# S5 layer of a decoder trunk: each group of channels gets its own 64x64 quarter of the array, and rows of u, K and y are moved by DMA through DRAM

## The chip, the cores and the metric

The kernel runs on one core of a Trainium2 chip. The metric is the device time of one execution, in microseconds (us).

## The reference, cut to what matters

The trunk has two layers over 256 positions of 2048 channels. The second layer's mixer runs a sliding-window attention beside an S5 state-space layer. S5 has 64 groups of 16 channels; each group has 64 complex states of its own, so no group reads another group's channels:

```python
u32 = u.reshape(b, s, 64, 16)                                  # 64 groups of 16 channels
a_bar = exp(lam * dt);  b_bar = ((a_bar - 1) / lam) * b_mat    # per group: 64 states
bu = einsum('bsgc,gpc->bsgp', u32, b_bar)                      # complex
state = linear_scan(a_bar, bu)                                 # over the positions
y = einsum('bsgp,gcp->bsgc', state, c_mat).real + d_skip * u32
z = gelu(y)
return z * sigmoid(z @ glu_w + glu_b)
```

Everything else (projections, attention, the other layer, the two feed-forward blocks) is dense work that the change leaves as it is.

## The kernel before, in words

**Dense work.** Each projection runs in groups. A group loads its weights as 1 MB tiles `w` on the one DMA queue that the kernel uses, that of SyncE (SP), from a pool of six buffers (`WB`) that the `ada` tiles share. ScalarE (ACT) rounds each half of a tile to `hi` (L330), VectorE (DVE) takes the rest as `lo` (L331), four buffers of each, and TensorE (PE) runs three matmuls for each 128x128 piece (helper `mm`, L138): hi times the activation's high part, hi times its low part, lo times its high part. One group of the odd layer's input projection has 96 of these matmuls, one of its output projection or of the GLU 48. A `step` emits a group and then what belongs beside it: DVE's work on the `ada` tiles, and chains of smaller work that advance one piece per slot. A scheduler turns this into one fixed instruction order for each engine before the run; each engine then works strictly in that order, and so does each DMA queue.

**S5.** Four positions are handled at a time: u is regrouped so that a partition is a position in the block of four and a channel, 32 channels (two groups) by 4 positions on 128 partitions, 64 blocks along the free axis. One unit i = 0 to 7 covers 128 channels as four sub-units t. All S5 matmuls are float32, with 128x128 weights that hold two groups of channels side by side; the other group's half of each is zero. A float32 matmul shows in the trace as two records.
- `s5_tables` (L1125) makes the weights of unit i from the parameters, during the first layer's feed-forward block (`ffn(0)`): powers of A on DVE, masked copies on ACT (L1151, L1152, L1163), eight transposes (L1171) copied by L1172, twelve matmuls with 32 columns, and ten copies of 32 partitions (L1188) that lay out the convolution kernel K. L836 spills the five tables of a unit to DRAM, 256 KB each, on SP's queue.
- `s5_states` (L1210) runs eight matmuls with 64 columns for unit i, then a chain of fourteen DVE operations (two scans among them) that gives `hs`, the states.
- `s5_outputs` (L1249) runs twelve matmuls on u, `hs` and the tables and copies the result to `y` (L1259).
- `s5_load` regroups u by sixteen ACT copies of 32 partitions (L939) for each pair of units; `s5_store` does the same from y to z (L961). L972 brings six tables of a unit back, on SP's queue.
- `s5_all` issues, in slot n, the table loads of unit n, the states of unit n-1 and the outputs of unit n-2. It starts when the first u is there. The odd input projection's groups come in the order `OD_ORDER = 'uqqqquuu'` behind the first (k and v), and the S5 work lies between their matmuls and those of the attention's output projection (`od_out`). Rows of a query group are moved between partitions by four DMAs (L585).

After the attention's part of `od_out`, z goes through a gelu (L1003) and is split into high and low part (L318, L319); then come the GLU's four groups, which read all eight pieces of z in order, and the S5 half of `od_out`.

Of the kernel before, what the change touches and what calls it, by code (L numbers as in the profile page):

```python
# [27 lines left out]
U_DMA = False  # L28
Z_DMA = False
# [66 lines left out]
def trunk(ctx: ExitStack, tc: tile.TileContext, a: dict, out: bass.AP):  # L96
# [525 lines left out]
    s5d = [[dp.tile([P, 512], F32, name=f"s5_{i}_{j}") for j in range(6)] for i in range(8)]  # L622
# [140 lines left out]
    for i in range(8):  # L763
        beside[steps[0] + TURN_AT[i]] = lambda i=i: DMA.dma_start(s5d[i][5], s5_turn(nc, s5w, i))
# [166 lines left out]

    def s5_load(g, ps):

        if not U_DMA:
            us[g] = t2((P, 2, 4, 64))
            un = ps.rearrange("p m (c j) -> p m j c", j=4)
            for t in range(4):
                for q in range(4):
                    S.copy(us[g][32 * q:32 * q + 32, :, t, :], un[32 * t:32 * t + 32, :, 3 - q, :])  # L939
# [6 lines left out]
    def turn_rows(src, dst, g):  # L946

        d = dp.tile([P, 2, 4, 64], F32, name=nm("rows"))
        DMA.dma_start(d, src)
        dst[g] = t2((P, 2, 4, 64))  # L950
        for b in range(4):
            DMA.dma_start(dst[g][32 * b:32 * b + 32], d.rearrange("(a r) m b c -> r b m a c", a=4)[:, b])

    def s5_store(g):
        if Z_DMA:
            turn_rows(ys[g], zs, g)
            return
        zs[g] = t2((P, 2, 4, 64))
        for t in range(4):
            for j in range(4):  # L960
                S.copy(zs[g][32 * t:32 * t + 32, :, j, :], ys[g][32 * j:32 * j + 32, :, t, :])  # L961

    def s5_all():

        tabs, hs = {}, {}
        for n in range(10):
            while n < 8 and n // 2 not in us:
                yield
            if n < 8:
                tabs[n] = [t2() for _ in range(6)]  # L970
# [74 lines left out]
def cmul(V, o_re, o_im, ar, ai, br, bi, tmp):  # L1045
# [79 lines left out]
def s5_tables(nc, w, i, pss, mm):  # L1125
    V, S, G, PE = nc.vector, nc.scalar, nc.gpsimd, nc.tensor
    t1, t2, sm, a, par, ident = (w[k] for k in ("t1", "t2", "sm", "a", "par", "ident"))
    ts = slice(4 * i, 4 * i + 4)

    def powers(k0, k1, x):  # L1130
# [13 lines left out]
    d = powers(1, 4, (craw[:, 0], craw[:, 1]))  # L1144
    c0 = t1((P, 2, 4, 2, 16))
    ckf = [t2() for _ in range(2)]
    ck = [v.rearrange("p (t k e c) -> p t k e c", t=4, k=4, e=2) for v in ckf]
# [6 lines left out]
    b0, tmp = [sm((P, 4, 16)) for _ in range(2)], sm((P, 4, 16))  # L1154
    fr, fi = (w["f"][:, r, ts].unsqueeze(2).to_broadcast([P, 4, 16]) for r in (0, 1))
    cmul(V, b0[0], b0[1], fr, fi, craw[:, 2], craw[:, 3], tmp)
    d = powers(1, 3, b0)
    bk = []
    for r in range(2):
        S.copy(d[r][:, :, 0, :], b0[r])  # L1160
# [226 lines left out]
```

## Time and profile before

| | before |
|---|---|
| median of 3 runs | 2244.04 us (2243.14 to 2247.28) |
| the profiled execution's own time | 2243.86 us |
| its span in the trace | 2242.0 us |
| PE / PE's weight loads / DVE / ACT busy | 97% / 88% / 83% / 56% |
| mean granted TensorE clock | 0.985 of full speed |
| DMA, mean busy share, and rate | 73.3%, 274 GB/s |

The profiled execution takes 1.86 us more than its span, and lies inside the three runs. A busy share is a mean over stages with different limits. PE's records are pipelined and overlap, so the step from one record's start to the next (its pitch), not its duration, is what it takes of PE's time.

### The profile page before, as it was taken

How to read it: one execution, taken by the hardware profiler on the slowest of the kernel's cores; microseconds unless marked ns; L12 is line 12 of the kernel's file. 1: busy time of each engine (PE TensorE's matmuls, PEld its weight loads, DVE VectorE, ACT ScalarE, POOL GpSimd, SP SyncE). 2: the span in 40 equal slices, each digit the busy share in tenths (PEclk: the TensorE clock that was granted, in tenths of full speed). 3: DMA queues.
4: the chain of work that ended last, by engine and by line, in shares of the span. 5: the costliest groups of instructions: out<-in, count | busy, mean ns of one | idle time of the engine just before them, and what ended most of it. 6: DMA issues, size and time to landing. Idle time of an engine off the chain costs nothing. (4 is left out here: it accounts for less than half of the span.)

```text
span 2242.0 us, 36822 instructions
## 1 busy us (share of the span) xinstructions
PE 2181.0 (97%) x14266; PEld 1981.4 (88%) x14266; DVE 1867.4 (83%) x3104; ACT 1257.1 (56%) x2188; POOL 4.4 (0%) x12
## 2 busy tenths in 40 slices
PE   7999999999999999999999999999999999999997
PEld 4799989998988888888888999999989888888886
DVE  7789999989999869999988778986799757877765
ACT  3355856445776456655544777644566444555543
POOL 0000000000000000000000000000000000000000
PEclk9999999999999999999999999999999999999999
DMA  8997689888768977788876757878755768655651
GB/s 341 383 347 295 237 310 354 323 351 302 283 228 307 359 300 311 305 322 333 326 283 202 288 210 270 301 242 294 291 188 203 258 228 307 244 188 188 205 195 71
DMA packets 106066, 615.05 MB, mean 274 GB/s; under 512 B 12065, under 2 KB 14625, under 8 KB 54817
## 3 DMA queue, kind: packets, MB, share of 16 engines
q1 hardware_dynamic: 105890, 612.69, 73.3%
q8 instruction: 112, 1.84, 0.3%
q14 instruction: 64, 0.52, 0.1%
HBM read 592.72 MB, written 18.87 MB: 273 GB/s over the span
## 5 line engine op out<-in xcount | busy, mean ns | idle before, releaser
L138 PE MATMUL mm<-t,hi 128*128 128x256 f32 (+1 forms) x4720 | 1213.5, 324 | 11.1 <-ACT hi L393 4.3
L138 PEld LDWEIGHTS mm<-t,hi 128*128 128x128 f32 x4720 | 795.3, 192 | 64.9 <-ACT hi L393 4.7
L138 PE MATMUL mm<-t,lo 128*128 128x256 f32 x3168 | 846.1, 285 | 3.6 <-DVE lo L331 3.5
L331 DVE TENSOR_TENSOR lo<-w,hi 128x1024 fp32r<-128x1024 f32 (+1 forms) x558 | 654.6, 1183 | 188.2 <-ACT hi L330 177.8
L330 ACT CAST hi<-w 128x1024 fp32r<-128x1024 f32 (+1 forms) x558 | 561.9, 1017 | 419.6 <-PE sp L138 268.4
L138 PE MATMUL sp<-t,hi 128*128 128x512 f32 (+1 forms) x2448 | 789.2, 357 | 0.0
L138 PEld LDWEIGHTS mm<-t,lo 128*128 128x128 f32 x3168 | 606.7, 192 | 24.0 <-DVE lo L331 5.5
L138 PE MATMUL sp<-t,lo 128*128 128x256 f32 x2032 | 523.4, 283 | 0.0
L138 PEld LDWEIGHTS sp<-t,hi 128*128 128x128 f32 x2448 | 436.9, 190 | 53.3 <-ACT hi L393 0.2
L221 DVE CUSTOM_DVE_ANT_0 ada<-ada,cond 128x2048 f32<-128x2048 f32 x192 | 438.4, 2285 | 10.5 <-DMA ada<-in_adaT 6.5
L138 PEld LDWEIGHTS sp<-t,lo 128*128 128x128 f32 x2032 | 389.0, 192 | 16.4
L393 ACT CAST hi<-w 128x768 fp32r<-128x768 f32 (+2 forms) x160 | 146.8, 922 | 168.7 <-PE sx L138 89.3
L394 DVE TENSOR_TENSOR lo<-w,hi 128x768 fp32r<-128x768 f32 (+2 forms) x160 | 167.7, 1062 | 63.3 <-ACT hi L393 61.0
L797 DVE SCALAR_TENSOR_TENSOR t<-t,ffn_p,t 128x255 f32<-128x255 f32 (+1 forms) x344 | 148.8, 480 | 11.3 <-ACT t L795 9.5
L795 ACT ACTIVATE t<-t,ffn_p 128x256 f32<-128x256 f32 x172 | 93.5, 594 | 51.8 <-DVE t L787 43.7
L291 ACT ACTIVATE t<-t,mods 128x256 fp32r<-128x256 f32 x64 | 30.0, 506 | 84.1 <-DVE mods L311 61.8
L138 PE MATMUL sx<-t,t 128*128 128x64 f32 (+2 forms) x480 | 68.3, 283 | 2.4 <-DMA t<-s 1.3
L138 PEld LDWEIGHTS sx<-t,t 128*128 128x128 f32 x480 | 61.8, 194 | 4.7 <-DMA t<-s 1.6
L318 ACT CAST t<-t 128x256 fp32r<-128x256 f32 x102 | 40.3, 404 | 42.9 <-DVE t L801 36.6
L138 PE MATMUL mm<-t,w 128*128 128x256 f32 x256 | 56.5, 380 | 0.9 <-ACT t L695 0.9
L264 ACT ACTIVATE t<-x 128x256 f32<-128x256 f32 x80 | 31.8, 414 | 44.3 <-DVE x L469 25.7
L138 PEld LDWEIGHTS mm<-t,w 128*128 128x128 f32 x256 | 48.5, 190 | 7.8 <-ACT t L695 1.3
(272 smaller groups left out, 1525.7 us busy)
## 6 DMA issues: line engine op xcount, KB each, us to landing
ada<-in_adaT SPq DMA_DIRECT2D x192, 1024.0 KB, 6.1
w<-in_ffn_in SPq DMA_DIRECT2D x116, 1024.0 KB, 5.6
w<-in_ffn_out SPq DMA_DIRECT2D x80, 896.0 KB, 4.6
w<-in_ffn_first SPq DMA_DIRECT2D x48, 896.0 KB, 6.1
w<-in_ev_out SPq DMA_DIRECT2D x16, 1024.0 KB, 6.5
w<-in_ffn_out SPq DMA_DIRECT2D x16, 1024.0 KB, 5.1
w<-in_od_out SPq DMA_DIRECT2D x16, 1024.0 KB, 6.9
w<-in_ev_a SPq DMA_DIRECT2D x16, 896.0 KB, 6.7
```

The costliest lines, as they stand in the source:

```text
L138: keep(PE.matmul(o, l, r, start=start, stop=stop, skip_group_check=True))
L221: V.tensor_tensor_reduce(out=w, in0=w, in1=cond, scale=1.0, scalar=0.0, op0=ALU.mult, op1=ALU.add, accum_out=mods[l][:, j:j + 1])
L264: S.activation(sq, x[i], AF.Square)
L291: S.activation(o[:, 0, :], t, AF.Identity, bias=sh[:, i:i + 1])
L318: S.copy(o[:, 0, :], src)
L330: S.copy(hi[:, :m], w[:, o:o + m])
L331: V.tensor_tensor(lo[:, :m], w[:, o:o + m], hi[:, :m].bitcast(F32), op=ALU.subtract)
L393: S.copy(hi[:, :c], w[:, o:o + c])
L394: V.tensor_tensor(lo[:, :c], w[:, o:o + c], hi[:, :c].bitcast(F32), op=ALU.subtract)
L795: S.activation(c, ps[s], AF.Identity, bias=fp[:, 3, j:j + 1], scale=fp[:, 2, j:j + 1])
L797: V.scalar_tensor_tensor(c[:, d:], ps[s][:, :T - d], fp[:, 2 - d, j:j + 1], c[:, d:], op0=ALU.mult, op1=ALU.add)
```

## The change

Every S5 matmul is cut into 64x64 quarters: one group's rows against one group's columns, for the upper half (partitions 0 to 63) and the lower half (64 to 127) in turn. There are twice as many S5 matmuls for states and outputs, each a quarter of the size. The zero halves are gone, so the tables take 512, 512, 256 and 512 columns in place of six times 512. Rows no longer lie in 32s that ACT can copy between partitions; u and y are written whole to DRAM and read back by eight DMAs of 16 partitions each (`turned`), and K is written as 128x112 and copied inside DRAM by sixteen DMAs for each unit. ACT makes four copies of 128 partitions for u and none for y.

```diff
     def s5_table(i):
-        tabs = yield from s5_tables(nc, s5w, i, psx, mm)
-        for d, t in zip(s5d[i], tabs):
-            DMA.dma_start(d, t)
+        bT, c5, kz = yield from s5_tables(nc, s5w, i, psx, mm)
+        DMA.dma_start(s5d[i][0], bT)
+        for r in range(2):
+            DMA.dma_start(s5d[i][1].rearrange("p (r t s) -> p r t s", r=2, t=4)[:, r],
+                          c5[r][:, :, 1:5, :].rearrange("p t k c -> p t (k c)"))
+
+        zd = dp.tile([P, 112], F32, name=nm("kz"))
+        DMA.dma_start(zd, kz.rearrange("p k c -> p (k c)"))
+        dst = s5d[i][2].rearrange("(e q c) (t s) -> q t e c s", e=2, q=4, t=4)
+        src = zd.rearrange("(t e c) s -> t e c s", t=4, e=2)
+        for q in range(4):
+            for t in range(4):
+                DMA.dma_start(dst[q, t], src[t, :, :, 16 * q:16 * q + 64])
...
+    def turned(src, view, dst, rows):
+
+        d = dp.tile([P, 2, 4, 64], F32, name=nm("rows"))
+        DMA.dma_start(d, src)
+        v = d.rearrange(view, r=16, **rows)
+        for n in range(8):
+            DMA.dma_start(dst[16 * n:16 * n + 16], v[n // v.shape[1], n % v.shape[1]])
+
     def s5_load(g, ps):

...
         un = t2((P, 2, 4, 64))
         for q in range(4):
             S.copy(un[:, :, q, :], ps.rearrange("p m (c j) -> p m j c", j=4)[:, :, 3 - q, :])
-        turn_rows(un, us, g)
...
+        us[g] = t2((P, 2, 4, 64))
+        turned(un, "(t e r) m q c -> e q r m t c", us[g], dict(t=4, e=2))
 
     def s5_store(g):
-        if Z_DMA:
-            turn_rows(ys[g], zs, g)
-            return
         zs[g] = t2((P, 2, 4, 64))
-        for t in range(4):
-            for j in range(4):
-                S.copy(zs[g][32 * t:32 * t + 32, :, j, :], ys[g][32 * j:32 * j + 32, :, t, :])
+        turned(ys[g], "(e j r) m t c -> t e r m j c", zs[g], dict(e=2, j=4))
...
     def s5_all():
...
-                tabs[n] = [t2() for _ in range(6)]
+                tabs[n] = [t2()[:, :v.shape[1]] for v in s5d[n]]
...
 def s5_tables(nc, w, i, pss, mm):
...
         for e in range(2):
-            m = par[:, 1 + r, e:e + 1]
-            S.activation(ck[r][:, :, :, e, :], d[r], AF.Copy, scale=m)
-            S.activation(c0[:, r, :, e, :], craw[:, r], AF.Copy, scale=m)
...
-    for r in range(2):
-        S.copy(d[r][:, :, 0, :], b0[r])
-        o = t2((P, 4, 4, 2, 16))
-        for e in range(2):
-            S.activation(o[:, :, :, e, :], d[r], AF.Copy, scale=par[:, 1, e:e + 1])
-        bk.append(o)
+            S.activation(bp[:, r, :, e, :], b0[r], AF.Copy, scale=par[:, 1, e:e + 1])
     for _ in range(YIELDS):
         yield
-    bT = [t2() for _ in range(2)]
+
+    tp = pss().rearrange("p (r t s) -> p r t s", r=2, t=4)
     for r in range(2):
-        tp = pss()
         for t in range(4):
-            PE.transpose(tp[:, t * P:(t + 1) * P], bk[r][:, t].rearrange("p k e c -> p (k e c)"), ident)
-        S.copy(bT[r], tp)
-
-    dd = sm((P, 4, 32))
-    V.tensor_tensor(dd, w["eye"].unsqueeze(1).to_broadcast([P, 4, 32]),
-                    w["d"][:, ts].unsqueeze(2).to_broadcast([P, 4, 32]), op=ALU.mult)
-    kps = pss().rearrange("p (t c) -> p t c", t=4)
-    for t in range(4):
-        mm(kps[:, t, 0:32], ident, dd[:, t, :], True, False)
-        for r in range(2):
-            mm(kps[:, t, 0:32], bk[r][:, t].rearrange("p k e c -> p (k e c)"),
-               c0[:, r, t].rearrange("p e c -> p (e c)"), False, r == 1)
-    kTf = t2()
-    kT = kTf.rearrange("p (t j c) -> p t j c", t=4, j=4)
-    G.memset(kTf, 0.0)
-    for k in range(4):
-        for q in range(k, 4):
-            S.copy(kT[32 * q:32 * q + 32, :, k + 3 - q, :], kps[32 * k:32 * k + 32, :, 0:32])
-    return *bT, *ckf, kTf
+            for h in (slice(0, 64), slice(64, 128)):
+                mm(tp[h, r, t, :], bk[r][h, t].rearrange("p k c -> p (k c)"), ident[h, h], True, True)
+    bT = t2()
+    S.copy(bT.rearrange("p (r t s) -> p r t s", r=2, t=4), tp)
+
+    kps = pss()
+    for r in range(2):
+        for t in range(4):
+            mm(kps[32 * t:32 * t + 32, 0:64], bp[:, r, t].rearrange("p e c -> p (e c)"),
+               c5[r][:, t, 0:4, :].rearrange("p k c -> p (k c)"), r == 0, r == 1)
+    kz = sm((P, 7, 16))
+    G.memset(kz[:, 0:3, :], 0.0)
+    V.scalar_tensor_tensor(kz[:, 3, :], w["eye"], w["d"][:, i:i + 1], kps[:, 0:16], op0=ALU.mult, op1=ALU.add)
+    S.copy(kz[:, 4:7, :].rearrange("p k c -> p (k c)"), kps[:, 16:64])
+    return bT, c5, kz
...
 def s5_states(nc, w, i, u, tabs, pss, mm, pin):
...
     for r in range(2):
         for t in range(4):
-            mm(vps[:, r, t, :], bT[r][:, t, :], u[:, t, :], True, True)
+            for h in (slice(0, 64), slice(64, 128)):
+                mm(vps[h, r, t, :], bT[h, r, t, :], u[h, t, :], True, True)
...
 def s5_outputs(nc, u, tabs, hs, y, pss, mm, pin):
...
     for t in range(4):
-        mm(yps[:, t, :], kT[:, t, :], u[:, t, :], True, False)
+        for h in (slice(0, 64), slice(64, 128)):
+            mm(yps[h, t, :], kT[h, t, :], u[h, t, :], True, False)
         for r in range(2):
-            mm(yps[:, t, :], ck[r][:, t, :], hs[:, r, t, :], False, r == 1)
+            for h in (slice(0, 64), slice(64, 128)):
+                mm(yps[h, t, :], ck[h, r, t, :], hs[h, r, t, :], False, r == 1)
     nc.scalar.copy(y, yps)
```

The scheduler lays out the whole program again. Three places follow.

**First place: PE, the input projection.** `mm_` is a group of 96, `sx_` an S5 result, `sp_` an attention score; the operand behind the arrow is what streams, then the weights; x4 is four such rows in a row. Before, the first states (unit 0) stand behind 7 matmuls of the third query group:

```order
L138 MATMUL mm_12714<-t_2053_12627,lo_12831 128x256
L138 MATMUL mm_12972<-t_1975_12153,hi_12975 128x256 x2
L138 MATMUL mm_12972<-t_1975_12153,lo_12976 128x256
L138 MATMUL mm_12972<-t_1975_12153,hi_12975 128x256 x2
L138 MATMUL mm_12972<-t_1975_12153,lo_12976 128x256
L138 MATMUL mm_12972<-t_1980_12184,hi_12975 128x256
L138 MATMUL sx_12899<-t_2065_12697,t_2075_12784 128x64 x4
L138 MATMUL mm_12972<-t_1980_12184,hi_12975 128x256
L138 MATMUL sp_12796<-t_2061_12677,t_2072_12773 128x128
```

Now, in a listing whose lines are two less, they stand behind 51 matmuls of the fourth:

```order
L136 MATMUL mm_13169<-t_1955_12332,lo_13177 128x256
L136 MATMUL mm_13169<-t_1960_12363,hi_13295 128x256 x2
L136 MATMUL mm_13169<-t_1960_12363,lo_13296 128x256
L136 MATMUL sx_12849<-t_2010_12661,t_2021_12742 64x64 x7
L136 MATMUL sp_12750<-t_2005_12636,t_2018_12731 128x128
L136 MATMUL sp_12750<-t_2005_12636,t_2018_12731 128x256
L136 MATMUL sp_12764<-t_2005_12636,t_2018_12731 128x128
L136 MATMUL sp_12764<-t_2005_12636,t_2018_12731 128x256
L136 MATMUL sx_12849<-t_2010_12661,t_2021_12742 64x64 x9
```

The first S5 work has moved back by about 140 dense matmuls.

**Second place: PE, from `od_out` to the GLU.** Before, the outputs of unit 7 (`sx_14724`) lie inside the sixth group of `od_out` (`mm_14823`), and 132 dense matmuls follow before the GLU:

```order
L138 MATMUL sx_14724<-t_2324_14269,t_2357_14472 128x64
L138 MATMUL sx_14724<-t_2381_14636,t_2355_14470 128x64
L138 MATMUL sx_14724<-t_2381_14636,t_2356_14471 128x64
L138 MATMUL sx_14724<-t_2324_14269,t_2357_14472 128x64
L138 MATMUL sx_14724<-t_2381_14636,t_2355_14470 128x64
L138 MATMUL sx_14724<-t_2381_14636,t_2356_14471 128x64
L138 MATMUL mm_14823<-t_2164_13288,hi_14826 128x256 x2
L138 MATMUL mm_14823<-t_2164_13288,lo_14827 128x256
```

Now the last group of `od_out` (`mm_15012`) is followed at once by the states of unit 6 (`sx_14504`, on u of units 6 and 7, `t_2265`) and the outputs of unit 5 (`sx_14541`):

```order
L136 MATMUL mm_15012<-t_2221_13974,lo_15020 128x256
L136 MATMUL mm_15012<-t_2221_13974,hi_15019 128x256 x2
L136 MATMUL mm_15012<-t_2221_13974,lo_15020 128x256
L136 MATMUL sx_14504<-t_2265_14282,t_2273_14352 64x64 x16
L136 MATMUL sx_14541<-t_2230_14044,t_2252_14192 64x64 x2
L136 MATMUL sx_14541<-t_2283_14394,t_2251_14191 64x64 x4
```

and then by the states of unit 7 and the outputs of units 6 and 7 (`sx_14777`), behind which the GLU (`mm_15105`, on z's first piece `t_2361`) follows at once:

```order
L136 MATMUL sx_14777<-t_2265_14282,t_2295_14493 64x64 x2
L136 MATMUL sx_14777<-t_2320_14677,t_2294_14492 64x64 x4
L136 MATMUL mm_15105<-t_2361_15078,hi_15108 128x256
L136 MATMUL mm_15170<-t_2361_15078,hi_15173 128x256
L136 MATMUL mm_15105<-t_2361_15078,hi_15108 128x256
L136 MATMUL mm_15105<-t_2361_15078,lo_15109 128x256
L136 MATMUL mm_15105<-t_2361_15078,hi_15108 128x256 x2
```

The tail of S5, from the states of unit 6 to the outputs of unit 7, has no dense matmul between its parts any more.

**Third place: SP's queue.** Before, the tables of unit 6 (`s_6_`) and those of unit 7 stand between weight loads:

```order
L972 DMA t_2314_14197<-s_5_5_1438 128x512
L324 DMA w_14824<-in_od_out 128x2048
L972 DMA t_2331_14345<-s_6_0_1439 128x512
L972 DMA t_2332_14346<-s_6_1_1440 128x512
L972 DMA t_2333_14347<-s_6_2_1441 128x512
L972 DMA t_2334_14348<-s_6_3_1442 128x512
L972 DMA t_2335_14349<-s_6_4_1443 128x512
L972 DMA t_2336_14350<-s_6_5_1444 128x512
L219 DMA ada_14885<-in_adaT 128x2048
L972 DMA t_2353_14468<-s_7_0_1445 128x512
```

Now y of units 2 and 3 goes out and comes back as z (`t_2262`), then u of units 6 and 7 (`t_2265`), and only then come the tables of unit 6:

```order
L944 DMA rows_14267<-t_2243_14105 128x512
L217 DMA ada_15167<-in_adaT 128x2048
L947 DMA t_2262_14266<-rows_14267 16x8x64 x8
L944 DMA rows_14283<-t_2264_14277 128x512
L322 DMA w_15171<-in_glu 128x2048
L947 DMA t_2265_14282<-rows_14283 16x8x64 x8
L970 DMA t_2273_14352<-s_6_0_1434 128x512
L970 DMA t_2274_14353<-s_6_1_1435 128x512
L970 DMA t_2275_14354<-s_6_2_1436 128x256
L970 DMA t_2276_14355<-s_6_3_1437 128x512
```

Each of the two turns has a weight load or `ada` load between its write and its eight reads, and the reads wait for the write to land.

## Rows read from the trace of the kernel before

**Rows 1.** The page's part 1: busy time, share of the span, instructions.

```profile
PE 2181.0 (97%) x14266; PEld 1981.4 (88%) x14266; DVE 1867.4 (83%) x3104; ACT 1257.1 (56%) x2188; POOL 4.4 (0%) x12
```

**Rows 2.** Windows: length; PE, PEld, DVE, ACT, POOL busy; granted clock; DMA share, GB/s.

```profile
600.00:1000.00 400.00, 390.52 (x2364) 347.30 (x2364) 356.42 (x609) 247.25 (x484) 4.21 (x8) 0.98 0.79 303
1240.00:1280.00 40.00, 38.02 (x289) 35.64 (x288) 27.92 (x68) 29.28 (x76) 0.00 (x0) 0.91 0.67 248
1280.00:1420.00 140.00, 139.31 (x1166) 132.67 (x1165) 112.82 (x283) 104.33 (x291) 0.00 (x0) 1.00 0.65 248
1420.00:1440.00 20.00, 20.00 (x169) 20.00 (x169) 19.90 (x27) 10.08 (x15) 0.00 (x0) 1.00 0.84 309
```

**Rows 3.** Groups by line and form, PE: S5's matmuls over the whole span.

```profile
L138 PE MATMUL sx<-t,t 128*128 128x64 f32 x320 | 40.3, 275 | 1.5 <-DMA t<-s 1.3
L138 PE MATMUL sx<-t,t 128*128 128x32 f32 x128 | 19.7, 278 | 0.0
L138 PE MATMUL sx<-sm,pack 128*128 128x32 f32 x64 | 12.4, 276 | 0.6 <-ACT t L1172 0.6
L1171 PE MATMUL sx<-pack,t 128*128 128x128 f32 x64 | 9.1, 275 | 1.5 <-ACT t L1163 1.5
```

**Rows 4.** Timeline of PE's weight loads: start, length, kind, records.

```profile
1316.17 0.31 PEld L138 LDWEIGHTS mm<-t,hi 128*128 128x128 f32 x2
1316.41 0.19 PEld L138 LDWEIGHTS mm<-t,lo 128*128 128x128 f32 x1
1316.53 4.55 PEld L138 LDWEIGHTS sx<-t,t 128*128 128x128 f32 x40
```

**Rows 5.** The same view, around attention heads that use half of the array.

```profile
1280.98 0.56 PEld L138 LDWEIGHTS sp<-t,t 64*128 64x128 f32 x8 [0.27 <-issue]
1281.87 0.90 PEld L138 LDWEIGHTS sp<-t,t 128*64 128x64 f32 x12 [0.33 <-issue]
1282.95 0.30 PEld L138 LDWEIGHTS mm<-t,hi 128*128 128x128 f32 x2 [0.17 <-issue]
1283.38 0.85 PEld L138 LDWEIGHTS sp<-t,t 64*128 64x128 f32 x8
```

**Rows 6.** Timeline of PE and its weight loads: waits around S5's first uses.

```profile
628.16 0.58 PE L138 MATMUL mm<-t,lo 128*128 128x256 f32 x1 [1.98 <-DVE lo L331]
...
1253.36 0.97 PEld L138 LDWEIGHTS sx<-t,t 128*128 128x128 f32 x8 [1.55 <-DMA t<-s]
```

**Rows 7.** Timeline of ACT: one unit's K copies, and the last units' y and z.

```profile
626.27 2.65 ACT L1188 COPY t<-sx 32x128 f32<-32x128 f32 x10 [1.28 <-PE sx L138]
...
1407.74 0.38 ACT L1259 COPY t<-sx 128x256 f32<-128x256 f32 x1 [2.91 <-PE sx L138]
1408.15 4.92 ACT L961 COPY t<-t 32x128 f32<-32x128 f32 x16
...
1416.84 0.63 ACT L1003 ACTIVATE t<-t 128x512 f32<-128x512 f32 x1
```

**Rows 8.** Timeline of DVE: first, twelfth and last operation of unit 7's chain.

```profile
1396.62 0.42 DVE L1228 TENSOR_TENSOR t<-sx,t 128x256 f32<-128x256 f32 x1
...
1400.44 0.41 DVE L1241 TENSOR_TENSOR t<-t,t 128x252 f32<-128x252 f32 x1
...
1404.69 0.41 DVE L1245 TENSOR_TENSOR t<-t,t 128x252 f32<-128x252 f32 x1
```

**Rows 9.** Groups by form in 600 to 1000, ACT: the weights' casts and their waits.

```profile
L330 ACT CAST hi<-w 128x1024 fp32r<-128x1024 f32 x112 | 114.8, 1048 | 53.3 <-PE sp L138 27.9 <-DMA w<-in_ffn_out 11.9 <-DMA w<-in_ffn_in 7.1
```

**Rows 10.** SP's waits: line, waits for, us in total, times, longest.

```profile
SPq L836 <- ACT t L1172: 52.8, 9, 11.2
SPq L836 <- ACT t L1188: 34.7, 8, 5.0
SPq L836 <- ACT t L1151: 18.7, 9, 5.9
```

**Rows 11.** Timeline of SP: issues, four of 32 partitions and six of 128.

```profile
1247.82 2.50 SPq L585 DMA_DIRECT2D t<-t  x4
1250.42 2.93 SPq L972 DMA_DIRECT2D t<-s  x6
```

**Rows 12.** DMA issues: count, KB each, median us from issue to landing.

```profile
w<-in_glu SPq DMA_DIRECT2D x4, 1024.0 KB, 6.7
s<-t SPq DMA_DIRECT2D x48, 256.0 KB, 2.7
t<-s SPq DMA_DIRECT2D x48, 256.0 KB, 6.9
t<-t SPq DMA_DIRECT2D x16, 64.0 KB, 2.0
```

More of the change, by code (lines that the diff above doesn't have):

```diff
@@ L27 @@
 C_DMA = True
-U_DMA = False
-Z_DMA = False
 HB = 4
@@ L621, in trunk @@
     dp = ctx.enter_context(tc.tile_pool(name="dp", bufs=1, space=bass.MemoryType.DRAM))
-    s5d = [[dp.tile([P, 512], F32, name=f"s5_{i}_{j}") for j in range(6)] for i in range(8)]
+    s5d = [[dp.tile([P, n], F32, name=f"s5_{i}_{j}") for j, n in enumerate((512, 512, 256, 512))] for i in range(8)]
     def spill_x():
@@ L763, in trunk @@
     for i in range(8):
-        beside[steps[0] + TURN_AT[i]] = lambda i=i: DMA.dma_start(s5d[i][5], s5_turn(nc, s5w, i))
+        beside[steps[0] + TURN_AT[i]] = lambda i=i: DMA.dma_start(s5d[i][3], s5_turn(nc, s5w, i))
     out_proj("ev_out", 0, None if EV_OLD else gate, mix, EV_QUOTA[4])
@@ L1142, in s5_tables @@
     craw = t1((P, 4, 4, 16))
     nc.sync.dma_start(craw, a["s5_cb"][i])
[L1144 to L1147, printed above, removed]
+    c5 = [t2()[:, :320].rearrange("p (t k c) -> p t k c", t=4, k=5) for _ in range(2)]
+    powers(1, 4, (craw[:, 0], craw[:, 1]), [v[:, :, 1:5, :] for v in c5], True)
     for r in range(2):
-        for e in range(2):
-            m = par[:, 1 + r, e:e + 1]
-            S.activation(ck[r][:, :, :, e, :], d[r], AF.Copy, scale=m)
-            S.activation(c0[:, r, :, e, :], craw[:, r], AF.Copy, scale=m)
@@ L1154, in s5_tables @@
[L1154 to L1158, printed above, removed]
-    for r in range(2):
-        S.copy(d[r][:, :, 0, :], b0[r])
-        o = t2((P, 4, 4, 2, 16))
-        for e in range(2):
-            S.activation(o[:, :, :, e, :], d[r], AF.Copy, scale=par[:, 1, e:e + 1])
-        bk.append(o)
+        S.activation(c5[r][:, :, 0, :], craw[:, r], AF.Copy, scale=(1.0, -1.0)[r])
@@ new lines, in s5_tables @@
+    b0, btmp = [sm((P, 4, 16)) for _ in range(2)], sm((P, 4, 16))
+    fr, fi = (w["f"][:, r, ts].unsqueeze(2).to_broadcast([P, 4, 16]) for r in (0, 1))
+    cmul(V, b0[0], b0[1], fr, fi, craw[:, 2], craw[:, 3], btmp)
+    bk = [t1((P, 4, 4, 16)) for _ in range(2)]
+    powers(1, 3, b0, [v[:, :, 1:4, :] for v in bk], False)
+    bp = t1((P, 2, 4, 2, 16))
+    for r in range(2):
+        S.copy(bk[r][:, :, 0, :], b0[r])
+        for e in range(2):
+            S.activation(bp[:, r, :, e, :], b0[r], AF.Copy, scale=par[:, 1, e:e + 1])
@@ L1189, in s5_tables @@
-    return *bT, *ckf, kTf
+            for h in (slice(0, 64), slice(64, 128)):
[3 more added lines that the diff above has]
+    kps = pss()
+    for r in range(2):
+        for t in range(4):
+            mm(kps[32 * t:32 * t + 32, 0:64], bp[:, r, t].rearrange("p e c -> p (e c)"),
+               c5[r][:, t, 0:4, :].rearrange("p k c -> p (k c)"), r == 0, r == 1)
@@ L1249, in s5_outputs @@
 def s5_outputs(nc, u, tabs, hs, y, pss, mm, pin):
-    ck = [v.rearrange("p (t s) -> p t s", t=4) for v in tabs[2:4]]
-    kT = tabs[4].rearrange("p (t s) -> p t s", t=4)
+    ck = tabs[1].rearrange("p (r t s) -> p r t s", r=2, t=4)
+    kT = tabs[2].rearrange("p (t s) -> p t s", t=4)
     pin()
```

38 lines of the change are left out of this document (15 added, 23 removed).

## The prediction, before the run

> **What bounds the kernel now.** I read the busy shares first: PE is busy 97% of the span [rows 1]. Then the windows of the two stages in which S5 works: while the tables are made PE is busy 390.52 of 400 us at a granted clock of 0.98, from 1240 to 1280 us 38.02 of 40 at 0.91, from 1280 to 1420 us 139.31 of 140 at 1.00, and in the GLU after that it does not pause [rows 2]. So PE sets the time in both; what the change is worth is how much of PE's path it removes, less what it makes PE wait. DVE and ACT have room, and SP's queue too, but PE sits behind all three in the S5 chain. There is little to win from waits: 9.5 us of idle and 8 us at the lower clock (400 x 0.02) in the first stage, 2.0 and 3.6 us (40 x 0.09) in the second, 0.7 in the third.
>
> **Term 1, PE's records.** A block of 40 S5 records lasts 4.55 us less one record's own overhang, and the dense matmuls ahead of it come at 0.12 us each [rows 4]; I take 0.11 us for a 128x128 float32 record whatever its columns. States and outputs are 320 records [rows 3], 35.2 us. The tables are 128, 64 and 64 records [rows 3], 256 in all, 28.2 us. After it, states and outputs have 640 records of a quarter's size, the tables 32 + 16 for each of 8 units, 384. No row shows a 64x64 record. The nearest are attention heads whose weights have 64 rows and 128 columns: where the two heads lie in opposite halves and both are ready, eight records take 0.56 us, 0.07 each; where one head comes alone, eight take 0.85, 0.11 each [rows 5]. Half the columns of both operands should halve that: 0.035 us for a record if upper and lower quarter run side by side, 0.055 if not. The order alternates upper and lower, and each pair has its own rows and columns, so I take 0.035, and keep 0.055 as a rival. A change of the array's shape shows as PE idle for 0.27, 0.33 and 0.17 us without any releaser [rows 5]; I take 0.28. States and outputs stand in eight blocks after the change, 16 changes; a table has about three, 24 in all.
> - States and outputs: 640 x 0.035 + 16 x 0.28 = 26.9 against 35.2: -8.3.
> - Tables: 384 x 0.035 + 24 x 0.28 = 20.2 against 28.2: -8.0.
> - Together -16. If shape changes cost nothing it would be -28, if they cost 0.33 and nothing overlaps, +6.
>
> The Trainium skill, TensorEngine Tiling (Array Packing), Key Properties, says both that different tiles work in parallel and that a change of tiling mode drains TensorE. The trace agrees with both in the rows above: eight records in 0.56 us, and 0.17 to 0.33 us of idle at each change. By the first alone the sum would hold only its gain; by the second the gain is cut by 40 x 0.28 = 11 us, which is the form in which the sum has it.
>
> **Term 2, the start of S5.** Before, PE waits 1.55 us for the first tables [rows 6] and loses about 5.6 us in idle and clock from 1240 to 1280 us [rows 2]. Now the first states stand some 140 dense matmuls, 17 us, later (first place of the change), and tables and u have long landed by then, though u0 goes through DRAM. Not all of it was due to S5; I take -5 (0 to -5.6).
>
> **Term 3, ACT around the tables.** The ten K copies of a unit took ACT 2.65 us, and behind the first of them PE waited 1.98 us for the next weights' low part [rows 6, 7]. They go. Of the 17.5 us of idle and clock in that stage I give back a quarter: -4 (0 to -9).
>
> **Term 4, SP's queue in the table stage.** Now K's write must land before sixteen DMAs go out behind it on the same queue. A 256 KB spill landed in 2.7 us; issues of 32 partitions took 2.50 us for four, 0.6 each, those of 128 partitions 0.5 [rows 11, 12]; 2.7 + 16 x 0.4 to 0.6 is 9 to 12 us in which no weight load is issued, eight times. Before, SP already waited 52.8 + 34.7 + 18.7 = 106 us, 13 a unit, on the same tables' ACT work [rows 10], and PE lost little by it. But the weights are not always early there: the casts waited 11.9 + 7.1 = 19 us for weights to land [rows 9], and the DMA engines are 0.79 busy [rows 2], so a load lost is not quickly made up. I take +6 (0 to +25). A sentence from the pages against this change: the Trainium skill, DMA: Bandwidth & Descriptors, sets 512 B as the smallest transfer at line rate, and here every run is 256 B; no row times such a DMA apart, and the sum above goes by issue and landing.
>
> **Term 5, the head of `od_out`.** Units 2 and 3, with outputs 1 and 2, stand at its start with only 6 dense matmuls between them. Outputs 2 wait for the chain of unit 2 on DVE: its first twelve operations take 4.15 us, and three more follow [rows 8], 5.2 us without interruption, 6 to 8 with casts between. PE has about 4 us of other work in that time. And u of units 2 and 3, with its tables, lies behind weight loads on SP's queue. I take 7 us of idle and 3 for the clock, which after the 1.55 us wait cost 3.6 [rows 2, 6]: +10 (+3 to +15).
>
> **Term 6, the tail of S5.** This is the largest. Before, 132 dense matmuls (16 us at 0.12) covered everything behind the last outputs: the copy of y 0.38, the regrouping 4.92, the gelu 0.63 and the splits [rows 7]. Now nothing dense stands between the states of unit 6 and the GLU (second place). From the moment PE gets there:
> - u of units 6 and 7 and the tables of unit 6 are behind z's turn on SP's queue (third place): two writes that must land, two weight or `ada` loads and two times eight issues, 2 x (2.7 + 8 x 0.5), then the table's 6.9 us to landing (a turned row alone took 2.0) [rows 11, 12], some 20 us from the copy of y, of which PE has 12 us of matmuls, and part of the order runs side by side. Wait: 4 (0 to 8).
> - The chain of unit 6, then that of unit 7, on DVE: 5.2 each if undisturbed, 8.5 for unit 7 before [rows 8]. Two: 12.
> - Outputs 7 (48 records, 1.7), the copy of y 0.4, one gelu 0.6, one split 0.4: ACT has the splits of all pieces of z behind that copy, so the GLU's first matmul waits for it.
> - PE's own work meanwhile: 7.5 us.
>
> 4 + 1.4 + 12 + 1.7 + 1.4 = 20.5, less 7.5: 13 idle, and 3 for the clock: +16 (+8 to +24). The last pieces of z come about 7 us behind that copy; the GLU's first six pieces (36 matmuls a group, 13 us) cover them. ACT loses the copies of z (4.92 for each pair), which no longer matters to PE.
>
> **Sum.** -16 - 5 - 4 + 6 + 10 + 16 = +7. The profiled execution, 2243.86 us with its span of 2242.0, is within 0.2 us of the median; 2243.9 + 7 is 2251 us.
>
> **Rivals.**
> - *Waits shorter than I sum (faster).* The tail's price hangs on DVE: if u and the tables of unit 6 are there when PE arrives and both chains run undisturbed (10.4), the tail costs 7 with a clock that stays up; if the head of `od_out` finds its inputs in time, 3. With SP's term at 0: -16 - 5 - 4 + 0 + 3 + 7 = -15, 2229 us. It decides where terms 5 and 6 together cost less than 19 us (with SP's 6). For it: in that stage DMA is 0.65 busy, and 6.9 us of table loads for each unit were hidden [rows 2, 12]. Against: the order, which leaves PE no other work. 0.22.
> - *Quarters do not run side by side.* 0.055 for a record: states and outputs 35.2 + 4.5, tables 21.1 + 6.7, together 67.5 against 63.4, +4 in place of -16: 2271 us. For it: where weights have 64 columns and 128 rows, 12 records take 0.90, 0.075 each, more than half of 0.11 [rows 5]. Against: the 0.56 us row. 0.12.
> - *SP starves the weights.* If each unit's 9 to 12 us costs PE 3, term 4 is +24: 2269 us. For it: the casts' 19 us of waits. Against: 13 us a unit were hidden before. 0.14.
> - *The gains and the tail cancel.* Terms 5 and 6 at 19: 2244 us, no change. 0.22. The forecast itself, +5 to +17, has 0.30.
>
> **How the numbers follow.** A measurement of this kernel tells a change from none at about 0.2%, 4.5 us. Slower by more: forecast, quarters alone and SP, 0.56, less a little because the cases blur into their neighbours: 0.50. Within: 0.24. Faster: 0.26. The range takes in half of the faster rival and reaches to the two slow ones: 2232 to 2271. The forecast's own range is 2248 to 2261.
>
> **What the profile will show.** Term 1: the pitch of the 64x64 records, 0.035 or 0.055, and PE's idle without a releaser beside them. Terms 2 and 3: no wait for tables at the first states, and less idle in the table stage. Term 4: SP's waits for K's landing, and casts waiting for weights by more than 19 us. Terms 5 and 6: PE idle behind DVE's chain at the start of `od_out` and ahead of the GLU, with a clock below 1. If the GLU follows `od_out` with less than 5 us of idle, the forecast is wrong on the low side; if the records come at 0.055 or the casts wait 40 us, on the high side.

## The result and the profile after

The changed kernel takes 2295.54 us (median of 4 runs, 2294.83 to 2297.04) against 2243.59 of the kernel before: 2.2% slower, ratio 1.0224, 95% interval 1.0211 to 1.0236. The forecast was 2251 us, slower, with a range of 2232 to 2271; the direction was right and the size was not. Experiments 1 to 9 below are single runs. Sixteen runs of the kernel before on one chip lie between 2242.22 and 2249.07 us, so a difference of less than some 5 us between two single runs says nothing.

The page's part 1, to be set beside [rows 1]: PE has 8 us less to do and the span is 51 us longer, so PE waits for some 60 us more.

```profile
PE 2173.0 (95%) x14714; PEld 1964.4 (86%) x14714; DVE 1872.5 (82%) x3109; ACT 1180.5 (51%) x1948; POOL 1.3 (0%) x12
```

The windows (columns as in [rows 2]) say in which stages.

```profile
600.00:1000.00 400.00, 364.03 (x2423) 319.74 (x2422) 346.60 (x591) 195.49 (x347) 0.97 (x7) 0.96 0.71 273
1264.59:1304.59 40.00, 39.00 (x349) 37.38 (x348) 25.50 (x61) 21.42 (x46) 0.00 (x0) 1.00 0.55 196
1360.00:1400.00 40.00, 29.88 (x321) 26.79 (x320) 28.04 (x81) 17.73 (x57) 0.00 (x0) 0.83 0.67 229
1440.00:1480.00 40.00, 26.79 (x316) 25.78 (x316) 26.16 (x58) 9.56 (x21) 0.00 (x0) 0.70 0.69 226
```

In the table stage PE is busy 364.03 of 400 us where it was 390.52. The start of the input projection lies at 1264.59 to 1304.59 here, where it lay at 1240 to 1280; PE idles 1.0 us there where it idled 2.0, and the granted clock is 1.00 where it was 0.91. Then come two holes of 10 and 13 us with a granted clock of 0.83 and 0.70, at the head of `od_out` and ahead of the GLU.

Three marks cut the run into pieces that every kernel here has: the first convolution activation of `ffn(0)` (L795; L794 after), the first copy of k for the attention heads (the first 64x256 copy on ACT), and the end of the span.

| us | first mark | to the k copy (table stage) | from there to the end (mixer and rest) |
|---|---|---|---|
| before | 538.1 | 702.9 | 1001.0 |
| after | 542.6 | 723.0, +20.1 | 1027.7, +26.7 |

The first mark is 4.5 us later; among the kernels below it lies between 537.5 and 541.9, and I did not follow that up. The table stage takes 674.6 to 681.5 us in the ten kernels below that issue K's DMAs from POOL and alternate the quarters, so a stage too varies by some 7 us.

### The profile page after: what moved, and what is told of

It reads as the page before. It is cut to its first block, busy times and chain, and to the rows that moved or that the text cites. A ratio compares the mean times of both kernels' runs of the same rounds, so it can differ in the third digit from the quotient of the medians.

```text
span 2293.3 us, 37629 instructions
## 1 busy us (share of the span) xinstructions
PE 2173.0 (95%) x14714; PEld 1964.4 (86%) x14714; DVE 1872.5 (82%) x3109; ACT 1180.5 (51%) x1948; POOL 1.3 (0%) x12
## 5 line engine op out<-in xcount | busy, mean ns | idle before, releaser
L794 ACT ACTIVATE t<-t,ffn_p 128x256 f32<-128x256 f32 x172 | 93.8, 595 | 54.1 <-DVE t L786 49.1
L316 ACT CAST t<-t 128x256 fp32r<-128x256 f32 x102 | 40.4, 404 | 53.9 <-DVE t L800 49.1
L136 PE MATMUL sx<-t,t 64*64 64x64 f32 (+2 forms) x800 | 42.4, 259 | 22.1 <-DMA t<-s 14.2
L136 PEld LDWEIGHTS sx<-t,t 64*64 64x64 f32 (+2 forms) x800 | 35.5, 161 | 27.1 <-issue 16.0
L799 ACT ACTIVATE t<-t 128x256 f32<-128x256 f32 x86 | 35.7, 415 | 40.4 <-DVE t L796 40.2
```

Of the source, the lines that this page charges most:

```text
L136: keep(PE.matmul(o, l, r, start=start, stop=stop, skip_group_check=True))
L316: S.copy(o[:, 0, :], src)
L794: S.activation(c, ps[s], AF.Identity, bias=fp[:, 3, j:j + 1], scale=fp[:, 2, j:j + 1])
L799: S.activation(cv[0], cv[0], AF.Gelu_apprx_tanh)
```

## The table stage: who waits for whom

PE's waits (line, waits for, us in total, times, longest). The first row is that of the kernel before, the two others are those after; all nine waits of the second row lie in the table stage:

```profile
PE mm L138 <- ACT hi L330: 3.8, 4, 1.6
PE mm L136 <- ACT hi L328: 33.7, 9, 10.9
PE sx L136 <- DMA t<-s: 14.2, 3, 6.7
```

ACT makes `hi` late, in part because weights land late. Its casts, beside [rows 9] (11.9 + 7.1 us behind DMA), now wait 22.1 + 11.5 us for weights:

```profile
L328 ACT CAST hi<-w 128x1024 fp32r<-128x1024 f32 x107 | 109.3, 1048 | 57.9 <-DMA w<-in_ffn_out 22.1 <-PE sp L136 15.5 <-DMA w<-in_ffn_in 11.5
```

Weights are also issued late. SP's timeline around the first units' K:

```profile
624.73 0.34 SPq L322 DMA_DIRECT2D w<-in_ffn_first_rest  x1
626.88 0.33 SPq L834 DMA_DIRECT2D s<-t  x1
627.30 0.37 SPq L840 DMA_DIRECT2D kz<-sm  x1
...
630.74 0.33 SPq L217 DMA_DIRECT2D ada<-in_adaT  x1
632.09 9.59 SPq L845 DMA_DIRECT2D s<-kz  x16
641.79 0.34 SPq L322 DMA_DIRECT2D w<-in_ffn_in  x1
652.69 0.33 SPq L834 DMA_DIRECT2D s<-t  x1
```

Between the weight load at 624.73 and the next at 641.79 lie 17 us, 9.6 of them the sixteen copies at 0.6 each. Then SP stands until the next unit's first table can be spilled (652.69), and the load after that comes at 654.74. PE's longest wait ends at 660.45, with ACT's casts just before it:

```profile
659.04 0.40 ACT L316 CAST t<-t 128x256 fp32r<-128x256 f32 x1 [2.46 <-DVE t L800]
659.36 2.94 ACT L328 CAST hi<-w 128x1024 fp32r<-128x1024 f32 x3
660.45 0.80 PE L136 MATMUL mm<-t,hi 128*128 128x512 f32 x1 [10.87 <-ACT hi L328]
```

The cast that ends this wait did not itself wait for a weight. It stands on ACT behind a cast of activations (L316), which waited for DVE. So the trace alone does not lead from SP's queue to this wait; what ties the two together are the experiments.

Three experiments change in the source only what is done with K. In each the order of S5's blocks on PE from the input projection to the GLU is that of the changed kernel. In the table stage, though, the scheduler lays out SP, ACT and DVE anew each time: with K on POOL it puts three weight loads between the first unit's spill at L834 and the next unit's, where the changed kernel has one (641.79). Each run therefore shows the price of K's DMAs on SP together with that of the order laid around them. No run separates the two.

**1. No layout of K.**

```diff
-        zd = dp.tile([P, 112], F32, name=nm("kz"))
-        DMA.dma_start(zd, kz.rearrange("p k c -> p (k c)"))
...
-                DMA.dma_start(dst[q, t], src[t, :, :, 16 * q:16 * q + 64])
+        kf = kz.rearrange("p k c -> p (k c)")
+        for o, n in ((0, 112), (112, 112), (224, 32)):
+            DMA.dma_start(s5d[i][2][:, o:o + n], kf[:, :n])
```

> The changed kernel without the layout of K: each unit's K goes to its table by three plain spills of SBUF rows (112, 112 and 32 columns); no write to DRAM is waited for and the sixteen copies are left out, so the K values are not laid out. The order on PE stays as in the changed kernel. Theory A (in the table stage SP's queue, held by K's landing and sixteen issues, brings the weights late): the dense matmuls' lag on the kernel before grew by 19 us over that stage and, with the quarters' records 15 us cheaper, should shrink by 15 instead: 2295 - 34 = about 2261 us, within 8. Theory B (the waits there come from the table's chain on ACT and DVE, or from its new place among the weights): the lag stays, above 2285.

Measured: 2254.56 us, beside 2248.48 of the kernel before on the same chip. The table stage takes 685.1 us, 38 less than in the changed kernel and 18 less than before; the rest of the run 1027.1, as in the changed kernel. That is theory A's range, far from B's.

**2. The landing kept, three copies in place of sixteen.**

```diff
-        for q in range(4):
-            for t in range(4):
-                DMA.dma_start(dst[q, t], src[t, :, :, 16 * q:16 * q + 64])
+        for o, n in ((0, 112), (112, 112), (224, 32)):
+            DMA.dma_start(s5d[i][2][:, o:o + n], zd[:, :n])
```

> As the changed kernel, K's write to DRAM and the wait for its landing kept, but three copies of 128 partitions inside DRAM in place of sixteen of 32 runs (K is not laid out). If the sixteen issues (0.6 us each, 9.4 us a unit) are what holds the weights back, 2263 to 2272 us, close to the kernel without the copies. If the wait for the landing holds them (about 2 to 3 us a unit), 2285 to 2295.

Measured: 2259.64 us, 5 more than without the wait, 36 less than with sixteen copies, and 3 below the range that I gave. It is mainly the sixteen copies, not the landing, for which SP waited 8.9 us over all eight units of the changed kernel.

**3. K's DMAs on POOL's queue.**

```diff
-        DMA.dma_start(zd, kz.rearrange("p k c -> p (k c)"))
+        G.dma_start(zd, kz.rearrange("p k c -> p (k c)"))
...
-                DMA.dma_start(dst[q, t], src[t, :, :, 16 * q:16 * q + 64])
+                G.dma_start(dst[q, t], src[t, :, :, 16 * q:16 * q + 64])
```

> The changed kernel with K's write and its sixteen copies issued by GpSimd (POOL), whose queue is otherwise empty; the same transfers, complete work. Theory A: SP is free, 2261 to 2270 us. Theory B, or a load of the DMA engines by the 256-byte runs: 2285 or more.

Measured: 2246.86 us (2248.48 before on that chip): 49 us under the changed kernel, below the range I gave, with the same transfers. The window and the POOL rows of this kernel:

```profile
600.00:1000.00 400.00, 394.35 (x2647) 349.46 (x2646) 376.25 (x622) 218.86 (x381) 81.44 (x143) 0.99 0.85 310
```

```profile
624.54 0.71 POOL L840 DMA_DIRECT2D kz<-sm  x1 [343.32 <-ACT t L316]
630.22 9.40 POOL L845 DMA_DIRECT2D s<-kz  x16 [4.97 <-DMA kz<-sm]
```

POOL needs as long for the first unit's sixteen copies as SP did (9.40 and 9.59 us); for the other units they take 9.8 to 12.9 us, with pauses between them. But no weight load queues behind them: PE is busy 394.35 of 400 us at a granted clock of 0.99. The stage takes 678.9 us, 44 less than in the changed kernel, 24 less than before. The 256-byte runs themselves, 16 x 32 for each unit, are still moved and cost PE nothing that shows, so it was not the transfer but the place in the queue that PE paid for. The casts still wait 14.5 + 11.7 us for weights here, more than the 19 before, and yet PE does not lose by it: that sum is no measure of what PE pays. The Trainium skill, DMA: Bandwidth & Descriptors, Specifications, gives 512 B as the smallest transfer at line rate. No run here times these transfers apart.

This kernel beats the one without the layout by 8 us, 6 of them in the table stage, about what two single runs differ by. If there is a difference, I only argue its reading: the three plain spills there still stand on SP behind ACT's copy of K.

## The quarters on PE

PE's weight loads around the first unit's table, after (columns as in [rows 4]):

```profile
622.32 0.31 PEld L136 LDWEIGHTS mm<-t,hi 128*128 128x128 f32 x2
622.77 1.01 PEld L136 LDWEIGHTS sx<-pack,t 64*64 64x64 f32 x32
623.85 0.27 PEld L136 LDWEIGHTS sx<-t,t 128*32 128x32 f32 x16
624.21 0.30 PEld L136 LDWEIGHTS mm<-t,hi 128*128 128x128 f32 x2
```

32 records take 1.01 us, about 0.031 each; the blocks of 80 in experiment 5 come at 0.030. Two dense matmuls from 622.32 on take 0.24, so the next was due at 622.56. It comes at 624.21: this table costs PE 1.65 us with its changes of shape. Eight like it make 13.2, where the prediction, from [rows 3, 4], made 28.2 for the tables before. Not every unit's table lies in one block, so 13.2 is an estimate.

**4. All upper quarters first, then all lower ones** (K on POOL):

```diff
-    for r in range(2):
-        for t in range(4):
-            for h in (slice(0, 64), slice(64, 128)):
+    for h in (slice(0, 64), slice(64, 128)):
+        for r in range(2):
+            for t in range(4):
                 mm(vps[h, r, t, :], bT[h, r, t, :], u[h, t, :], True, True)
```

and so in outputs and transposes.

> K on POOL, and in states, outputs and transposes all upper quarters first, then all lower ones; the rest of the order stays. If neighbouring records run side by side only where upper and lower alternate, the 64x64 records' pitch rises from 0.030 to about 0.055 us, 896 records cost some 22 us more, part of it hidden in the waits: 2256 to 2269 us. If the pitch does not depend on the alternation (each record is simply short), 0.030 us and 2245 to 2249 us.

Measured: 2265.1 us, 18 more than with K on POOL alone. The same view of its first table:

```profile
618.34 1.76 PEld L136 LDWEIGHTS sx<-pack,t 64*64 64x64 f32 x32
```

1.76 us for 32 records, 0.055 each: close to the two prices of the forecast, one for each order. 0.024 us x 256 is 6.1 us for the tables and x 640 is 15.4 for states and outputs; the stages took 5.8 (684.6 against 678.9) and 15.1 us (1040.6 against 1025.5) longer. So close an agreement is in part luck, since a stage varies by some 7 us; the two pitches are the firmer evidence. The same records are cheaper where the quarters alternate. The Trainium skill, TensorEngine Tiling (Array Packing), Key Properties, says that different tiles can run their weight loads and matmuls in parallel; the two pitches agree with it.

## The mixer: the turns of u and y

With K on POOL the table stage is 24 us shorter than before, but the mixer and the rest take 1025.5 us, 24 us longer. In the changed kernel PE waits for tables at the head of `od_out`, in the states of unit 2:

```profile
1382.85 3.93 PE L136 MATMUL sx<-t,t 64*64 64x64 f32 x80 [6.74 <-DMA t<-s]
```

The tail, in the same view:

```profile
1444.50 0.28 PE L136 MATMUL mm<-t,lo 128*128 128x256 f32 x1
1451.45 6.44 PE L136 MATMUL sx<-t,t 64*64 64x64 f32 x116 [6.67 <-DMA t<-s]
1459.13 0.33 PE L136 MATMUL sx<-t,t 64*64 64x64 f32 x4 [1.25 <-DVE t L1239]
1460.13 2.09 PE L136 MATMUL sx<-t,t 64*64 64x64 f32 x44 [0.66 <-DVE t L1242]
1464.08 0.48 PE L136 MATMUL sx<-t,t 64*64 64x64 f32 x4 [1.86 <-DVE t L1239]
1464.87 2.40 PE L136 MATMUL sx<-t,t 64*64 64x64 f32 x40 [0.31 <-DVE t L1242]
1469.73 1.04 PE L136 MATMUL mm<-t,hi 128*128 128x256 f32 x3 [2.46 <-ACT t L316]
```

From the last dense matmul of `od_out` (1444.50) to the GLU's first (1469.73) are 25 us. The waits come in the order that the forecast had: the tables behind u's turn, the two chains of states on DVE (L1239, L1242), the splits of z (L316). PE's own records take 11.7 us of the 25, and the granted clock lies between 0.50 and 0.76 from 1445 to 1470 us. On SP:

```profile
1432.20 0.32 SPq L944 DMA_DIRECT2D rows<-t  x1
1432.64 0.36 SPq L217 DMA_DIRECT2D ada<-in_adaT  x1
1434.44 6.11 SPq L947 DMA_DIRECT2D t<-rows  x8
1440.66 0.53 SPq L944 DMA_DIRECT2D rows<-t  x1
1441.28 0.38 SPq L322 DMA_DIRECT2D w<-in_glu  x1
1443.14 5.07 SPq L947 DMA_DIRECT2D t<-rows  x8
1448.32 1.60 SPq L970 DMA_DIRECT2D t<-s  x3
```

Each turn holds SP for about 8 us; y's and u's take 16 together before the tables of unit 6 are issued at 1448.32, after PE has got there.

**5. Neither turned** (K on POOL): `us[g] = un`, `zs[g] = ys[g]`.

> K on POOL as in the third experiment, and u and y are not turned: the states read u as ACT copied it and z is y as the outputs left it (the rows are in the wrong places). On PE the S5 work then lies spread between dense matmuls again, the last outputs over 400 matmuls ahead of the GLU. With K on POOL the odd layer's mixer still lost 24 us on the kernel before, between the last dense matmuls of the feed-forward block and the GLU. Theory C (the turns through DRAM, by their time and the order that they force, cost what was lost): the loss turns into the quarters' gain, 24 + 13 less, 2247 - 37 = about 2210 us, within 8. Theory D (the chain of states on DVE, or the shape changes on PE): above 2235.

Measured: 2210.19 us (2245.16 before on that chip). The mixer and the rest take 987.2 us, 38 less than with the turns and 13.8 less than before, and PE does not pause between 1280 and 1400 us:

```profile
1280.00:1400.00 120.00, 120.00 (x1404) 113.02 (x1403) 112.72 (x254) 66.76 (x160) 0.00 (x0) 1.00 0.68 249
```

DVE has the same chains to run here, and PE does not wait for them once dense work lies around them. Theory D falls. Leaving out the turns also changes the order on PE, so this is the price of the turns and of the order that they force, together.

**6 and 7. One of them not turned** (K on POOL).

> K on POOL, y turned on SP as in the changed kernel, u not turned (the states read it as ACT copied it, its rows in the wrong places). Without both turns the gain against K on POOL alone was 37 us. If the turns of u, which the states and all behind them wait for, cost most: 2212 to 2222 us. If those of y, whose writes and reads stand ahead of the next u on SP's queue and whose z the GLU waits for: 2230 to 2245.

> K on POOL, u turned on SP, y not turned (z is y as the outputs left it, its rows in the wrong places). The counterpart of the run before it: 2230 to 2245 us if u's turns cost most, 2212 to 2222 if y's do. If each alone gives nearly all of the 37 us back, the cost is that of the two in one queue.

Measured: 2225.95 us without u's turns, 2227.98 without y's (2242.15 before on that chip), 21 and 19 us under K on POOL alone, which ran on another chip. Neither range of the expectation was met in either run. In the mixer and the rest they take 1008.8 and 1007.8 us, 17 and 18 less than K on POOL, where leaving out both took away 38: the two share the cost about evenly. Whether having both in one queue costs something on top, 3 or 4 us by these figures, single runs do not tell.

**8. The turns on POOL, K left on SP.**

```diff
-        DMA.dma_start(d, src)
+        G.dma_start(d, src)
...
-            DMA.dma_start(dst[16 * n:16 * n + 16], v[n // v.shape[1], n % v.shape[1]])
+            G.dma_start(dst[16 * n:16 * n + 16], v[n // v.shape[1], n % v.shape[1]])
```

> The changed kernel with the writes and reads of u and y issued by POOL; K stays on SP. The scheduler places S5's blocks somewhat differently between od_out's groups. Theory C (the waits at od_out's head and at the tail, 7.0 us each for tables behind the turns on SP's queue, come from the queue's order): these 14 us and part of the lower clock go, 2275 to 2283 us. Theory D (the chain of states on DVE and the order on PE make them): 2290 to 2298 us.

Measured: 2286.22 us, 9 less than the changed kernel, between C and D. The mixer and the rest take 1017.7 us, 10 less: taking the turns off SP's queue gives back a quarter of their 40 us, not all of it.

**9. Another order of the groups, all turns on SP** (K on POOL): `OD_ORDER = 'uquququq'` and `'uuqqquuq'`.

> K on POOL, u and y turned as in the changed kernel on SP, and the groups of the input projection in the order u q u q u q u q in place of u q q q q u u u: u of the last units is made two groups earlier, and on PE the last outputs lie in the fourth group of the attention's output projection, some 230 dense matmuls ahead of the GLU. Complete work. Theory C' (the turns cost little where dense matmuls lie behind them; it is their place ahead of the GLU that costs): 2215 to 2228 us. If the turns' own time or SP's queue costs in any place: 2238 to 2250. The last query group may now make the output projection wait, a few us.

> As the kernel before it, with the order u u q q q u u q. The same reading: 2215 to 2230 us by C', 2238 or more if the turns cost in any place.

Measured: 2262.7 and 2263.72 us, 16 and 17 more than with the old order and above both ranges that I gave. Theory C', that only the place ahead of the GLU costs, falls. PE's waits in the first of the two:

```profile
PE sp L139 <- ACT t L642: 18.0, 4, 5.9
...
PE sx L136 <- DVE t L1239: 10.6, 5, 3.4
PE sx L136 <- DMA t<-s: 8.2, 1, 8.2
```

The last outputs no longer stand right ahead of the GLU, but PE waits for three query groups' attention (L642), 5.7 to 5.9 us each time, and the row moves of these groups (L583) stand behind a turn on SP:

```profile
1327.68 0.32 SPq L944 DMA_DIRECT2D rows<-t  x1
1332.15 5.08 SPq L947 DMA_DIRECT2D t<-rows  x8
1337.34 2.46 SPq L583 DMA_DIRECT2D t<-t  x4
```

**10. All added DMAs on POOL**, with the old order, with `'uuqqqquu'`, with that and `U_S5 = 1000` (the scheduler puts S5 first), and with `'uquququq'`.

> All DMAs that the change added (K's write and copies, the writes and reads of u and y) on POOL's queue, groups in their old order, complete work. K on POOL gave 49 us, the rows on POOL 9 us in the odd layer's mixer. If they add up (two stages that do not meet): 2246.9 - 9 = about 2238 us (2232 to 2243), 0.3% under the kernel before. If POOL's slower issue or the shared DMA engines take it back: 2244 to 2250.

> As the kernel before it, with the input projection's groups in the order u u q q q q u u: on PE the last outputs lie 19 matmuls ahead of the end of the attention's output projection, and unit pairs 2 to 5 are spread over its groups. If the tail's cost is the lack of dense matmuls between its parts: 5 to 12 us under the kernel with the old order, 2226 to 2233. If the tail only moves on: the same 2238.

> As the kernel before it, and the scheduler puts S5's chain ahead of other work, so that 66 dense matmuls (8 us) follow the last outputs ahead of the GLU. If cover behind the last outputs is what is missing: 3 to 6 us under the kernel without the priority, 2221 to 2229. If S5 ahead of the weights' casts delays these: 2235 or more.

> The order u q u q u q u q of the sixth experiment, now with the turns of u and y on POOL too. There SP's queue held the attention's own row moves (L583) behind a turn, and PE waited 18 us for the attention's exponentials. If the queue did that: 2262.7 - 18 and some of the table's 8 us, 2235 to 2245. If the last query group's place at the end does it: 2255 to 2263.

| | median us | ratio to before | 95% interval |
|---|---|---|---|
| old order | 2238.59 | 0.9967 | 0.9955 to 0.9980 |
| u u q q q q u u | 2235.60 | 0.9952 | 0.9936 to 0.9968 |
| the same, S5 first | 2238.98 | 0.9975 | 0.9963 to 0.9987 |
| u q u q u q u q | 2239.76 | 0.9978 | 0.9965 to 0.9990 |

The old order came as expected, so the two savings add up. All four are faster than the kernel before, by 0.2 to 0.5%. The 5 to 12 us that I expected from covering the tail did not come: with the second order dense matmuls lie between the tail's parts, and from the k copy to the end PE idles 33.4 us where it idled 37.6 with the old order, but it is busy 982.8 us where it was 977.6. The intervals do not tell the first two apart. The third missed the gain too. It lies in the range that I gave if S5 delays the weights' casts, but its table stage takes only 3 us more than the second's (681.5 and 678.3), too little to show it. The fourth came in the range that I gave if SP's queue was to blame: POOL's queue gave 23 us (2262.7 to 2239.8), and the waits for L642 fell from 18.0 to 6.8 us, though the order on PE is another there as well. The waits that stay I put down to the turn's own length. POOL in the first of the four:

```profile
1352.27 0.58 POOL L944 DMA_DIRECT2D rows<-t  x1 [13.11 <-ACT t L1258]
1360.52 4.32 POOL L947 DMA_DIRECT2D t<-rows  x8 [7.67 <-DVE t L1229]
1366.87 0.58 POOL L944 DMA_DIRECT2D rows<-t  x1 [2.03 <-DMA t<-rows]
1371.69 4.32 POOL L947 DMA_DIRECT2D t<-rows  x8 [4.24 <-issue]
```

From a write's issue to the last read's are 7 to 13 us over this kernel's eight turns, and the reads must still land; y's and u's turns still follow each other in one queue. No run here moves the rows without a write to DRAM that must land first.

## Why the prediction was wrong

PE's windows from mark to mark (columns as in [rows 2]): the table stage before, after and with K on POOL, then the mixer and the rest after and in experiment 5.

```profile
538.08:1240.99 702.91, 689.61 (x4170) 614.34 (x4169) 635.14 (x1040) 416.08 (x744) 4.21 (x8) 0.99 0.79 296
542.55:1265.58 723.03, 678.99 (x4298) 599.67 (x4297) 638.21 (x1040) 371.19 (x616) 0.97 (x7) 0.97 0.75 281
540.73:1219.59 678.86, 669.45 (x4298) 594.46 (x4297) 633.53 (x1040) 371.90 (x615) 81.44 (x143) 0.99 0.82 300
1265.58:2293.30 1027.72, 981.46 (x6962) 898.03 (x6962) 762.06 (x1247) 532.87 (x897) 0.00 (x0) 0.97 0.64 223
1221.19:2208.40 987.21, 968.05 (x6962) 885.75 (x6962) 760.50 (x1247) 533.32 (x897) 0.00 (x0) 0.99 0.65 228
```

- **Term 4, SP's queue in the table stage, is the step that failed.** The hold was sized right: 9 to 12 us a unit were forecast, and SP shows 9.4 to 9.6 for the issues and 1.1 on the average for the landing. What it costs PE was set at +6 with a bound of +25; it is 44 us (723.0 against 678.9 with the same DMAs on POOL), 5.5 us a unit. PE idles 44.0 us in that stage and 9.4 with K on POOL; the other 9.5 are longer busy time. The argument that failed was that SP had already waited 13 us a unit for ACT without loss [rows 10], so that most of the new hold would be hidden too. SP still waits some 88 us for ACT's tables (at L834 and L840), and the new hold comes on top. How much of the 44 is the hold itself and how much the order that the scheduler lays around it stays open. That a late load is not made up because the DMA engines are 0.79 busy [rows 2] is not shown: with K on POOL they are 0.85 busy in the 600 to 1000 us window. The rival that named this mechanism had a chance of 0.14 and a price of 3 us a unit, both too low. The sign set for it, casts waiting 40 us for weights, was not reached either (33.6), so the sign was a poor one.
- **Term 1** had the mechanism and the price nearly right (0.035 a record, measured 0.031), and asked too much for the changes of shape: the tables save about 15 us, not 8. In experiment 5 the mixer and the rest save 13.8 us, where terms 1 and 2 summed 8.3 + 5; PE's idle time is the same as before there (19.2 and 19.6 us), so the saving lies in its busy time.
- **Term 2** holds: the start of the input projection has 1.0 us of idle and a clock of 1.00, 4.6 us of the 5.6 that it was worth.
- **Term 3**, -4: with K on POOL the table stage is 24 us shorter than before. PE idles 3.9 us less (13.3 and 9.4), which is the size of the term. Beside the 15 of the records that leaves 5 us in PE's busy time, which was not taken apart.
- **Terms 5 and 6** named the right waits in the right places, but +10 and +16 are too small: the turns cost 40 us in the changed kernel (1027.7 against 987.2). Of these, 27 are idle (46.3 against 19.2 us), where 7 + 13 were summed, and 13 are longer busy time, where 3 + 3 were put down for the clock. The tail's idle was met in sum, 13.2 us in the window from 1440 to 1480, with 6.67 for the tables where 4 was put and less for the two chains. What was too small there is PE's own work at the lower clock: 7.5 us in the forecast, 11.7 measured. At the head the idle is 10.1 us, not 7. A turn holds SP for 8 us, not 6.7.
- The first operations of a chain were misread in [rows 8]: the row called the twelfth is the eleventh, and it ends 4.23 us after the first began, not 4.15. That carries no weight.
- The sum by what was measured: -15 - 9 + 44 in the table stage, -13.8 + 40.5 in the mixer, +4.5 ahead of both, is +51, the difference of the two spans (2293.3 - 2242.0). It closes by its making, since the parts are differences of the same stages; the evidence is in the experiments.

## What to carry to other kernels

Count the issues on a queue, not only the bytes: here sixteen small DMAs for each unit held the queue that also feeds the weights for 9.6 us, and that cost PE more than the smaller matmuls saved, while the same DMAs on an idle queue cost nothing that showed. Before an added hold of a queue is written off as hidden, ask whether it replaces an old wait of that queue or comes on top of it, and try it from another queue. Small matmuls on two quarters of the array were worth it here because neighbours in PE's order lie in different quarters: at 0.055 us, twice as many records would take as long as the large ones at 0.11. A detour through DRAM between two dependent steps cost up to 40 us here; a free queue gave back 10 of them, and the orders tried to put dense work behind it gave nothing that showed.

## What the runs showed of the hardware

- PE's weight-load records of 64x64 float32 quarters: 0.031 us each where upper and lower quarter alternate, 0.055 where all of one quarter come first.
- A DMA of 32 runs of 256 B inside DRAM takes 0.6 us to issue on SP and 0.59 on POOL (sixteen in 9.59 and 9.40 us); a spill of 128x512 took SP 0.33.
- K's write of 128x112 and the first copy that waits for it: from issue to issue 1.6 to 4.8 us on SP over the eight units, 2.4 to 6.8 on POOL.
- After PE's wait of 6.67 us for the tables in the tail the granted clock is 0.50 from 1450 to 1455 us, the lower of its two levels (1.2 GHz).
